# Cross attention's values by seven block products, with the weights' block sums grown in SBUF

## The chip, the core and the metric

The kernel runs on one NeuronCore of a Trainium2 chip, as one program in one launch. The metric is the device time of that launch in microseconds, as a median of several runs. Beside it stands one execution taken by the hardware profiler.

The engines are named as in the profile: PE is the matrix engine (PEld its loading of the stationary operand), DVE the vector engine, ACT the scalar engine, POOL the general engine, SP the engine that here only issues DMAs.

## What is computed

One decoder layer on 256 tokens of width 1024, in float32:

```python
xn = rmsnorm(h, norm_mix_g)
q_a, k_a, v_a, q_b, f_b, i_b, og_b, g_a, g_b = split_cols(xn @ w_in)
y_a = moba_attention(q_a, k_a, v_a, positions) @ w_br_attn
y_b = hgrn2(q_b, f_b, i_b, og_b, lb) @ w_br_hgrn
h = h + (sigmoid(g_a) * y_a + sigmoid(g_b) * y_b) @ w_out
# cross attention with 256 memory tokens, 4 heads of 256
q = rmsnorm(h, norm_x_g) @ wq_x
kv = rmsnorm(mem, norm_mem_g) @ wkv_x          # keys: columns 0 to 1023, values: 1024 to 2047
h = h + (softmax(q k^T / 16) v) @ wo_x
# feed-forward, hidden width 2816
gu = rmsnorm(h, norm_ffn_g) @ w_ffn_in
h = h + (silu(gate) * up) @ w_ffn_out
out = rmsnorm(h, final_norm_g)
```

The change is in the line of `kv` (its values) and in what surrounds it.

## The kernel before

**Precision.** A float32 operand is split into a high part (`hi`, in the format that PE multiplies fast) and the rest (`lo`), and a product is three matmuls: hi by hi, hi by lo, lo by hi. For activations the halves are named `Mh, Ml` (memory), `h1h, h1l` (the normed residual), `oxh, oxl` (what attention gives), for weights `hi, lo`. ACT copies the high part, DVE subtracts it from the raw tile.

**Units of weights.** All weights lie in one array `w` of units of 128 x 2048 (1 MB), in the order of the list `ORDER`. A unit of kind "F" is 256 columns by the full depth of 1024; one of kind "T" is 512 columns by half the depth (`kh` 0 or 1). `prep()` loads the next unit from DRAM into one of three `raw` buffers (its DMA is issued on SP), makes `hi` in two pieces of 1024 on ACT and `lo` in two on DVE; there are three buffers of each. `nxt()` returns the unit that is due and prepares up to two ahead (`LEAD`).

**Products.** `gemm_f` takes an "F" unit: two groups of 16 matmuls that give a feature-major result (`psf`); `gemm_t` takes two "T" units: 2 x 24 matmuls that give both groups of 128 tokens (`pst`). Each ends with `tick()`, which advances background generators (`bg`) by a step, so that the vector work of another part and its few matmuls lie among the big products. PE's instructions run in the order of the program; the order on the other engines is made by a scheduler, except where `keep_in_program_order` or `issue_after` says otherwise.

**Cross attention.** The memory is scaled by its gain and split (`memory()`, tile `M2`) while the attention's output products run. After `w_out` come four chunks of keys (`gemm_f(M2, ...)`, into `kxh, kxl`, the subtraction on POOL), the first half of the values (`gemm_t`, `ev_vx(0)`), four chunks of queries, and the second half of the values (`ev_vx(1)`). One chunk of queries is one head: `scores(x)` gives its scores (`xs`), the softmax on DVE and ACT (`xp`), and two ticks later the turn of the probabilities (`xT`, then `ph, pl`). `pv(x)` multiplies with the values (`xo`, into `ox`). After all four heads come the four units of `wo_x`, for each group of tokens and each half of the columns (`pso`), added to the residual `H` by `add_h2`; then the mean of squares (`rstd_h2`, `hn`), and the turn of the normed residual (`turn_h2`, `h2T`, `h2g`).

**The feed-forward** already computes pairs of its column blocks with seven products of a quarter of the work, in Strassen's manner with Winograd's sums: the products are `P1` to `P7`, in the order `SEVEN`, accumulated in the banks `pqA`, `pqB`, `pqF`, with token sums `SS` made once by `token_sums()`. The weights' sums come from `block_sums()`: one of its steps runs at each tick; SP copies a block to a DRAM tile (`t1`, `t2`, `t3`, `t4`), POOL adds another block by an accumulating DMA (line 743). Its unit's halves are made by `halve()` (lines 1146 and 1151).

Of the kernel before, what the change touches and what calls it, by code (L numbers as in the profile page):

```python
# [42 lines left out]
def plan():  # L43
# [13 lines left out]
    order += tgroup("wkv_x", 1024)[:2]  # L57
    order += [("F", "wq_x", c * 256) for c in range(4)]
    order += tgroup("wkv_x", 1024)[2:]
    order += tgroup("wo_x", 0)  # L60
# [9 lines left out]
SEVEN = ("P1", "P2", "P6", "P7", "P5", "P3", "P4")  # L70

# [22 lines left out]
SPACING = 9  # L94
# [50 lines left out]
def build(tc, A, out):  # L145
    nc = tc.nc
    V, SC, G, PE, SY = nc.vector, nc.scalar, nc.gpsimd, nc.tensor, nc.sync
    with ExitStack() as ctx:
# [46 lines left out]

        def prep(tags=None, raw=None):
# [3 lines left out]
            if raw is None:  # L200
                raw = wr.tile([128, 2048], F32, name="raw", tag="raw")
            if tags is None:
                hi = wh.tile([128, 2048], F32R, name="hi", tag="hi")
                lo = wl.tile([128, 2048], F32R, name="lo", tag="lo")
            else:
                hi = big(tags[0], "hix", (128, 2048), F32R)
                lo = big(tags[1], "lox", (128, 2048), F32R)
# [6 lines left out]
            if sent == 1:  # L214
                SY.dma_start(raw, A["w"][i])
            for c in range(pieces):
# [5 lines left out]
                V.tensor_tensor(lo[:, a], raw[:, a], hi[:, a].bitcast(F32), op=ALU.subtract)  # L222
            ready[i] = (hi, lo)
# [5 lines left out]
        def nxt(lead=LEAD):  # L229
            i = at[0]  # L230
            at[0] += 1
            while made[0] <= min(i + lead, len(ORDER) - 1):
# [74 lines left out]
        def split(src, hi, lo, scale=None):  # L307
            if scale is None:
                SC.activation(hi, src, AF.Copy)
                V.tensor_tensor(lo, src, hi.bitcast(F32), op=ALU.subtract)  # L310
# [426 lines left out]
        def block(q, name):  # L737
            i, kh = {"11": (1, 0), "21": (1, 1), "12": (0, 0), "22": (0, 1)}[name]
            return A["w"][where["I", q + i, kh]]

        def block_sums():
# [8 lines left out]
            for g, q in enumerate(DOUBLES):  # L750
                t1, t2_, t3 = (dr.tile([128, 2048], F32, name="%s_%d" % (z, q)) for z in ("t1", "t2", "t3"))
                scr[q] = {"P5": t1, "P6": t2_, "P7": t3}
                i = SPACING * g
                at_step(i, lambda t=t3, q=q: tc.keep_in_program_order(SY.dma_start(t, block(q, "22"))))
                at_step(i + 6, lambda t=t1, q=q: tc.keep_in_program_order(SY.dma_start(t, block(q, "11"))))
                at_step(i + 4, lambda t=t3, q=q: add(t, q, "12"))
                at_step(i + 10, lambda t=t1, q=q: add(t, q, "12"))
                at_step(i + 8, lambda t=t2_, t3=t3: tc.keep_in_program_order(SY.dma_start(t, t3)))
                at_step(i + 12, lambda t=t2_, q=q: add(t, q, "11"))
                if g == 0:  # L760
                    t4 = dr.tile([128, 2048], F32, name="t4")
                    scr[q]["P4"] = t4
                    at_step(i + 16, lambda t=t4, t2_=t2_: tc.keep_in_program_order(SY.dma_start(t, t2_)))
                    at_step(i + 20, lambda t=t4, q=q: add(t, q, "21"))
# [184 lines left out]

        def memory():  # L950
# [3 lines left out]
            for k in range(8):  # L954
                split(raw[:, k], Mh[:, k], Ml[:, k], gv[:, V_MEM + k:V_MEM + k + 1])
# [11 lines left out]
        mg = memory()  # L967
        start(mg)
# [55 lines left out]
        drain(mg)  # L1024
# [19 lines left out]
        pp = big("P2", "pp", (128, 2, 4, 2, 256), F32R)  # L1044
        ph, pl = pp[:, 0], pp[:, 1]

        def ev_vx(c):
            def ev(t, ps):
                a = slice(c * 512, (c + 1) * 512)
                split(ps, vxh[:, t, a], vxl[:, t, a], mem["r"][:, t:t + 1])  # L1050
            return ev

        gemm_t((Mh, Ml), ev_vx(0))
        drain(h1g)

# [28 lines left out]
        for c in range(4):  # L1084
            gemm_f(H1, ev_sum(qxh, qxl, c))
            g = scores(c)
# [5 lines left out]
        oxh, oxl = ox[:, 0], ox[:, 1]  # L1092

        def pv(x):
# [5 lines left out]
            split(po, oxh[:, 2 * x:2 * x + 2], oxl[:, 2 * x:2 * x + 2])  # L1100

        for x in range(XH):
            for g in sg[:x + 2]:
                drain(g)
            pv(x)
# [400 lines left out]
```

## Time and profile before

| | |
|---|---|
| median of 3 runs | 612.17 us (612.1 to 612.2) |
| the profiled execution | 612.86 us, span 611.1 us |
| granted clock of PE | 0.998 |
| busy PE / PEld | 602.2 / 502.9 us |
| busy DVE / ACT / POOL | 448.9 / 373.1 / 110.0 us |
| HBM | 155.21 MB read, 34.60 MB written |

A row of a group or of the timeline has the start (if it is one instruction), the time, engine and line, the operation, the tiles written and read, shapes and type; in square brackets stands the time for which the engine was idle before it and what ended that. A matmul's time is its length in a pipeline: the next one starts before it ends. In a list of waits the columns are the total in us, how often, and the longest. Times are microseconds from the start of the span.

### The profile page before, as it was taken

Reading aid. Unit: us, or ns where it says so; the run is one execution under the profiler, and the core shown is the slowest. Engines: PE = TensorE matmul, PEld = TensorE weight load, DVE = VectorE, ACT = ScalarE, POOL = GpSimd, SP = SyncE. Lnnn points to the kernel's source line nnn. Section 1 sums busy time; section 2 is a strip of 40 time slices with the busy share of each in tenths; the row PEclk is TensorE's granted clock in tenths of the full one; section 3 lists DMA queues with packets and bytes.
Section 4 is the critical chain, followed back from the end, with each engine's and each line's share of the span. In section 5 each row is a group of like instructions: output and inputs, shape, how many; then the busy total and the mean of one; then the engine's idle time right before and its main releaser. Section 6 shows DMA issues by size and latency. Waiting matters only on the chain.

```text
span 611.1 us, 8304 instructions
## 1 busy us (share of the span) xinstructions
PE 602.2 (99%) x3093; PEld 502.9 (82%) x3093; DVE 448.9 (73%) x702; ACT 373.1 (61%) x603; POOL 110.0 (18%) x137
## 2 busy tenths in 40 slices
PE   8999999999999999999999999999999999999995
PEld 7888888888887887778888888888878888888884
DVE  7598867978756877658866566694896887878953
ACT  7695545333377676736447656684776667677732
POOL 3898100112200431000301403100000000000003
PEclk9999999999999999999999999999999999999999
DMA  8886688747995789957779778863949979796601
GB/s 346 348 305 197 217 252 327 246 139 285 322 257 220 242 260 285 330 203 317 275 216 308 233 280 225 253 215 132 351 158 335 369 267 391 235 383 220 248 2 69
DMA packets 21864, 156.79 MB, mean 257 GB/s; under 512 B 2752, under 2 KB 3392, under 8 KB 5312
## 3 DMA queue, kind: packets, MB, share of 16 engines
q1 hardware_dynamic: 18224, 134.46, 56.7%
q0 software_dynamic: 2880, 20.97, 17.4%
q10 hardware_dynamic: 720, 0.84, 0.4%
q8 instruction: 24, 0.39, 0.3%
q14 instruction: 16, 0.13, 0.1%
HBM read 155.21 MB, written 34.60 MB: 311 GB/s over the span
## 4 chain that ended last, share of the span: by engine, by line
PE 90%; DVE 5%; ACT 2%; issue 1%; POOL 0%; POOLq 0%; DVEq 0%; ACTq 0%
PE pst L262 13%; PE pst L264 13%; PE pst L263 13%; PE pqA L1311 8%; PE psf L283 7%; PE pqF L1311 4%; PE psf L284 4%; PE acc L264 3%; PE acc L263 3%; PE acc L262 3%; PE pqB L1311 2%; PE lp L637 2%; DVE lo L1151 1%; PE psg L538 1%; PE as L826 1%
## 5 line engine op out<-in xcount | busy, mean ns | idle before, releaser
L222 DVE TENSOR_TENSOR lo<-raw,hi 128x1024 fp32r<-128x1024 f32 (+1 forms) x128 | 156.5, 1233 | 56.5 <-ACT hi L221 56.1
L221 ACT ACTIVATE hi<-raw 128x1024 fp32r<-128x1024 f32 (+1 forms) x128 | 129.0, 1028 | 98.5 <-PE pst L264 79.3
L262 PE MATMUL pst<-hi,XX 128*128 128x512 f32 x224 | 90.4, 404 | 0.0
L264 PE MATMUL pst<-hi,XX 128*128 128x512 f32 x224 | 87.4, 390 | 0.0
L263 PE MATMUL pst<-lo,XX 128*128 128x512 f32 x224 | 87.3, 390 | 0.0
L264 PEld LDWEIGHTS pst<-hi,XX 128*128 128x128 f32 x224 | 42.0, 188 | 9.0
L262 PEld LDWEIGHTS pst<-hi,XX 128*128 128x128 f32 x224 | 42.1, 188 | 8.8 <-issue 0.7
L263 PEld LDWEIGHTS pst<-lo,XX 128*128 128x128 f32 x224 | 42.1, 188 | 7.9
L1151 DVE TENSOR_TENSOR lo<-raw,hi 128x2048 fp32r<-128x2048 f32 (+1 forms) x18 | 36.8, 2052 | 10.6 <-ACT hi L1146 10.5
L1146 ACT ACTIVATE hi<-raw 128x1024 fp32r<-128x1024 f32 x32 | 32.0, 1052 | 7.4 <-PE acc L264 5.3
L1151 DVE TENSOR_TENSOR lo<-rawx,hi 128x2048 fp32r<-128x2048 f32 x12 | 27.5, 2288 | 8.1 <-ACT hi L1146 8.1
L1146 ACT ACTIVATE hi<-rawx 128x1024 fp32r<-128x1024 f32 x24 | 24.1, 1051 | 5.9 <-PE acc L264 2.6
L1311 PE MATMUL pqA<-hi,SS 128*128 128x512 f32 x80 | 26.4, 390 | 0.0
L1180 POOL DMA_DIRECT2D b<-t x4 | 3.6, 894 | 124.3 <-DVE fu L1244 124.3
L264 PE MATMUL acc<-hi,hids 128*128 128x512 f32 x62 | 24.3, 392 | 0.7 <-DVE hids L310 0.7
L262 PE MATMUL acc<-hi,hids 128*128 128x512 f32 x62 | 24.4, 393 | 0.0
L263 PE MATMUL acc<-lo,hids 128*128 128x512 f32 x62 | 24.2, 390 | 0.0
L283 PE MATMUL psf<-H,hi 128*128 128x512 f32 x64 | 22.7, 398 | 0.0
L283 PE MATMUL psf<-M,hi 128*128 128x512 f32 x64 | 22.5, 394 | 0.0
L283 PE MATMUL psf<-XX,hi 128*128 128x512 f32 x64 | 22.4, 394 | 0.0
L743 POOL DMA_DIRECT2D t<-w x16 | 13.8, 878 | 46.7 <-DMA t<-w 32.1
L1151 DVE TENSOR_TENSOR lo<-b,hi 128x2048 fp32r<-128x2048 f32 x7 | 16.0, 2292 | 6.2 <-ACT hi L1146 6.2
(418 smaller groups left out, 1511.7 us busy)
## 6 DMA issues: line engine op xcount, KB each, us to landing
raw<-w SPq DMA_DIRECT2D x75, 1024.0 KB, 6.3
t<-w POOLq DMA_DIRECT2D x16, 1024.0 KB, 10.0
raw<-t SPq DMA_DIRECT2D x12, 1024.0 KB, 6.8
rawx<-w SPq DMA_DIRECT2D x10, 1024.0 KB, 7.2
rawx<-t SPq DMA_DIRECT2D x4, 1024.0 KB, 8.9
b<-w SPq DMA_DIRECT2D x4, 1024.0 KB, 9.3
b<-t POOLq DMA_DIRECT2D x4, 1024.0 KB, 8.5
raw<-w SPq DMA_DIRECT2D x4, 512.0 KB, 6.5
```

Of the source, the lines that this page charges most:

```text
L221: SC.activation(hi[:, a], raw[:, a], AF.Copy)
L222: V.tensor_tensor(lo[:, a], raw[:, a], hi[:, a].bitcast(F32), op=ALU.subtract)
L262: PE.matmul(ps, xh, h, start=first, stop=False)
L263: PE.matmul(ps, xh, l, start=False, stop=False)
L264: PE.matmul(ps, xl, h, start=False, stop=last)
L283: PE.matmul(ps, w[0][:, k, a], X2[:, :, k], start=k == 0, stop=False)
L284: PE.matmul(ps[:, 0], w[1][:, k, a], X2[:, 0, k], start=False, stop=k == 7)
L637: PE.matmul(ps[:, j], KS[:, a0 + j], QQ[:, a0 + j], start=True, stop=True)
L743: tc.keep_in_program_order(G.dma_start(t, block(q, name), accum_op=ALU.add, max_dma_last_dim=8192))
L1146: pin(SC.activation(hi[:, a], raw[:, a], AF.Copy))
L1151: pin(V.tensor_tensor(lo[:, a], raw[:, a], hi[:, a].bitcast(F32), op=ALU.subtract))
L1311: PE.matmul(ps, x[k], z[:, k], start=first and k == 0 and i == 0, stop=k == 3 and i == 2, skip_group_check=not first)
```

## The change

The values are computed as the feed-forward computes its pairs: with the 256 memory tokens as two halves, the depth of 1024 as two halves and the columns as two halves, there are seven products of 12 matmuls with 512 columns. The token sums (`SSm`) come from `mem_sums()`. The seven products stand among the key chunks, in the order `CROSS` (numbers 0 to 3 are key chunks, 4 to 7 query chunks); both halves of the values are complete before the first query chunk.

The weights' sums: P1 reads block 11 from a tile of its own (`b11`), to which block 12 is added for P5. A tile `b22` is loaded with block 22 at step 36 of `block_sums()`, gets block 12 at step 38 (P7 reads it), then block 11 after P7's halves are made (P6), then block 21 after P6's (P4). P2 and P3 read blocks 21 and 22. These additions are accumulating DMAs issued by POOL. The memory's scaled copy `mg` is now kept, made by eight more copies on ACT.

The steps of `block_sums()` for the feed-forward follow each other at a spacing of 7 instead of 9 ticks, with other distances inside. After the last query chunk there is no more unit of values: `pv(0)`, `pv(1)`, the scores of the last head, and then output products of the first 128 tokens by heads (`wo_part(t, c, x)`, six matmuls each) alternate with `pv(2)` and `pv(3)`. The first halves for the feed-forward and one low part are ordered behind named instructions (`turned_v`, `behind`).

```diff
+CROSS = (0, "P1", "P7", "P2", 1, "P6", 2, "P5", 3, "P3", "P4", 4, 5, 6, 7)
...
-SPACING = 9
+SPACING = 7
+HOME = (36, 38)
+T4 = (19, 23)
...
+        sums, grow = {}, {"P1": "12", "P7": "11", "P6": "21"}
...
+            if STREAM[i] in ("P1", "P5"):
+                if STREAM[i] == "P1":
+                    sums["1"] = big("B12", "b11", (128, 2048))
+                raw = sums["1"]
+            elif STREAM[i] in ("P7", "P6", "P4"):
+                raw = sums["3"]
...
+            if STREAM[i] in grow:
+                G.dma_start(raw, block("vx", grow[STREAM[i]]), accum_op=ALU.add)
...
-                split(raw[:, k], Mh[:, k], Ml[:, k], gv[:, V_MEM + k:V_MEM + k + 1])
+                SC.activation(mg[:, k], raw[:, k], AF.Copy, scale=gv[:, V_MEM + k:V_MEM + k + 1])
+                split(mg[:, k], Mh[:, k], Ml[:, k])
...
+        def product(ps, x, w, first):
+            xh, xl = x
+            for k in range(4):
+                for i, (x, z) in enumerate(((xh, w[0]), (xh, w[1]), (xl, w[0]))):
+                    PE.matmul(ps, x[k], z[:, k], start=first and k == 0 and i == 0, stop=k == 3 and i == 2,
+                              skip_group_check=not first)
+
+        SSm = big("P2", "SSm", (128, 2, 4, 4, 128), F32R)
+
+        def mem_sums():
+            a11, a12, a21, a22 = (mg[:, 4 * c:4 * c + 4, t * 128:(t + 1) * 128] for t in range(2) for c in range(2))
+            V.tensor_tensor(a22, a22, a21, op=ALU.subtract)
+            V.tensor_tensor(a21, a11, a21, op=ALU.subtract)
+            yield 1
+            put(SSm, 2, a21)
+            yield 1
+            s2 = t2("s2", (128, 4, 128))
+            V.scalar_tensor_tensor(s2, a22, -1.0, a11, op0=ALU.mult, op1=ALU.subtract)
+            V.scalar_tensor_tensor(a12, s2, -1.0, a12, op0=ALU.mult, op1=ALU.subtract)
+            put(SSm, 1, s2)
+            yield 1
+            put(SSm, 0, a22)
+            put(SSm, 3, a12)
...
-        for c in range(4):
-            gemm_f(M2, ev_sum(kxh, kxl, c))
...
-        gemm_t((Mh, Ml), ev_vx(0))
...
+        def cross_product(name):
+            if name == "P6":
+                drain(ms)
+            key = {"P1": "A", "P6": "A", "P5": "A", "P3": "A", "P2": "B", "P7": "F", "P4": "F"}[name]
...
+            product(ps, block_tokens((Mh, Ml), SSm, name), by_k(nxt(), 4), first)
...
+        for u in CROSS:
+            if u in SEVEN:
+                cross_product(u)
+                continue
+            if u < 4:
+                gemm_f(M2, ev_sum(kxh, kxl, u))
+                continue
...
+            gemm_f(H1, ev_sum(qxh, qxl, u - 4))
...
-        gemm_t((Mh, Ml), ev_vx(1))
...
-        for x in range(XH):
-            for g in sg[:x + 2]:
-                drain(g)
-            pv(x)
...
+        pv(0)
+        pv(1)
+        for f in later:
+            f()
+        later.clear()
+        drain(sg[2])
+        run(prep(("P0",)))
...
+        wo_part(0, 0, 0)
+        wo_part(0, 0, 1)
+        pv(2)
+        wo_part(0, 1, 0)
+        wo_part(0, 1, 1)
+        drain(sg[3])
+        with tc.issue_after(turned_v[2]):
+            run(prep(("B12", "B6")))
+        wo.append(by_k(ready.pop(i0 + 3), 4))
+        wo_part(0, 0, 2)
+        pv(3)
+        drain(bs)
+        wo_part(0, 1, 2)
...
-                pin(SC.activation(hi[:, a], raw[:, a], AF.Copy))
+                with tc.issue_after(turned_v[3]) if n == 0 else nullcontext():
+                    pin(SC.activation(hi[:, a], raw[:, a], AF.Copy))
...
-                pin(V.tensor_tensor(lo[:, a], raw[:, a], hi[:, a].bitcast(F32), op=ALU.subtract))
+                with tc.issue_after(behind[n]) if n in behind else nullcontext():
+                    pin(V.tensor_tensor(lo[:, a], raw[:, a], hi[:, a].bitcast(F32), op=ALU.subtract))
...
-                for kh in range(2):
-                    wo_part(ps, t, c, kh)
-                add_h2(t, c, ps)
+                for x in range(0 if t else 3, 4):
+                    wo_part(t, c, x)
+                add_h2(t, c, pso[t, c])
```

More of the change, by code (lines that the diff above doesn't have):

```diff
@@ L56, in plan @@
     order += [("F", "wkv_x", c * 256) for c in range(4)]
-    order += tgroup("wkv_x", 1024)[:2]
+    order += tgroup("wkv_x", 1024)
     order += [("F", "wq_x", c * 256) for c in range(4)]
-    order += tgroup("wkv_x", 1024)[2:]
-    order += tgroup("wo_x", 0)
+    order += [("T", "wo_x", c * 512, kh) for kh in range(2) for c in range(2)]
     for j in range(NF // 2):
@@ L70, with stream @@
 SEVEN = ("P1", "P2", "P6", "P7", "P5", "P3", "P4")
+CROSS = (0, "P1", "P7", "P2", 1, "P6", 2, "P5", 3, "P3", "P4", 4, 5, 6, 7)
+def stream():
+    n = next(n for n, u in enumerate(ORDER) if u[0] == "I")
+    k = [ORDER.index(("F", w, c * 256)) for w in ("wkv_x", "wq_x") for c in range(4)]
+    return list(range(k[0])) + [k[u] if isinstance(u, int) else u for u in CROSS] + list(range(k[7] + 1, n))
+STREAM = stream()
 def ffn_plan():
@@ L1336, in ffn_product @@
             ps = bank_of[key]
-            product(ps, name, w, first)
+            product(ps, block_tokens(X2, SS, name), w, first)
             if name == "P1":
```

163 lines of the change are left out of this document (99 added, 64 removed).

## The prediction

> **What bounds the kernel now.** I read the page's busy times and chain first, then the waits of PE, then PE's timeline around the edit, then the other engines there.
>
> ```profile
> PE 602.2 (99%) x3093; PEld 502.9 (82%) x3093; DVE 448.9 (73%) x702; ACT 373.1 (61%) x603; POOL 110.0 (18%) x137
> PE 90%; DVE 5%; ACT 2%; issue 1%; POOL 0%; POOLq 0%; DVEq 0%; ACTq 0%
> ```
>
> ```profile
> PE warm L359 <- DVE still L356: 1.6, 1, 1.6
> PE acc L264 <- DVE hids L310: 0.7, 1, 0.7
> PE xT L1080 <- DVE xp L1074: 0.2, 1, 0.2
> ```
>
> The first line is busy time by engine, the second the chain of work that ended last, the three others everything that PE ever waited for (total, times, longest). PE is the bound: an edit gains what it takes out of PE's own queue, plus at most the last two waits, and loses whatever new waits it gives PE. The profiled execution took 612.86 us for a span of 611.1; the median of the runs is 612.17. I sum against 612.86 and move the result by the 0.69 between them. About 0.2% (1.2 us) is what a measurement of this kernel can tell from no change.
>
> **The matmuls taken out.** The values `mem @ wkv_x[:, 1024:]` are four units of 24 matmuls; seven products are 12 each.
>
> ```profile
> L262 PE MATMUL pst<-hi,M x32: 387/389/482, 350.4 to 401.1; 128*128 128x512 f32 x32
> L263 PE MATMUL pst<-lo,M x32: 389/389/397, 350.6 to 401.4; 128*128 128x512 f32 x32
> L264 PE MATMUL pst<-hi,M x32: 388/389/397, 350.8 to 401.6; 128*128 128x512 f32 x32
> ```
>
> ```profile
> 463.74 2.72 PE pqA L1311 x12
> 466.46 2.72 PE pqF L1311 x12
> ```
>
> The first three rows are all matmuls of the values: 96. The other two, from the chain, are products of the FFN of the very form the change uses: 12 matmuls take 2.72 us back to back (0.227 each; the 389 ns is the pipelined length of one). 96 - 84 = 12 matmuls: **-2.72 us**, all on the path. The first output products by heads are the same 96 matmuls in another order: 0.
>
> **What the seven products need from DVE and ACT.** In the new order, all of them stand among the keys' chunks, before the first query chunk.
>
> ```profile
> 327.20:361.30 34.10, 34.10 (x188) 29.55 (x187) 20.24 (x29) 20.60 (x36) 9.84 (x10) 1.00 0.86 290
> ```
>
> ```profile
> L222 DVE TENSOR_TENSOR lo<-raw,hi x6: 1216/1222/1228, 380.9 to 397.6; 128x1024 fp32r<-128x1024 f32 x6
> L221 ACT ACTIVATE hi<-raw x6: 1042/1054/1062, 379.8 to 395.7; 128x1024 fp32r<-128x1024 f32 x6
> ```
>
> ```profile
> 359.55 0.75 DVE L313 SCALAR_TENSOR_TENSOR vxl<-pst,r_m,vxh 128x512 fp32r<-128x512 f32 x1
> 437.00 0.69 DVE L1325 TENSOR_TENSOR fc<-pqB,f 128x512 f32<-128x512 f32 x1 [0.36 <-PE pqB L1311]
> 446.82 0.68 DVE L1287 TENSOR_TENSOR SS<-s,SS 128x512 fp32r<-128x512 f32 x1
> ```
>
> The window is that stage before (keys and half of the values): length, then busy PE, PEld, DVE, ACT and POOL. It halves six units; the new stage has eleven, and lasts 34.10 + 36 x 0.227 = 42.3 us. DVE: 20.24 + 10 halves x 1.22 + four `SSm` lows x 0.68 + two token sums and three `fc` x 0.69 + two more `vxl` x 0.75 = 40.1 us. ACT gets ten `hi` x 1.05 and some 6 us of copies: about 37. So PE stays the bound of the stage, but DVE is within 2 us of it. Units are halved two ahead and I find each pair ready by a microsecond or more: 0, with a bound of 2 us above. The extra scale copies of the memory (eight on ACT) lie in the output products of attention, well before their use: 0.
>
> **The sums grown in SBUF.** P7, P6 and P4 read one tile, `b22`, each after one more accumulating load from POOL; P5 reads P1's tile after one. A load cannot be issued before both halves of the product before are made.
>
> ```profile
> 303.23 0.69 DVE L918 SCALAR_TENSOR_TENSOR tat<-tat,pst 128x512 f32<-128x512 f32 x1 [1.12 <-PE pst L264]
> 330.76 1.22 DVE L222 TENSOR_TENSOR lo<-raw,hi 128x1024 fp32r<-128x1024 f32 x1
> 327.20 0.48 PE L283 MATMUL psf<-M,hi 128*128 128x512 f32 x1
> 332.84 1.03 PE L1002 MATMUL h1T<-cst,H 128*128 128x128 f32 x8
> 333.63 0.48 PE L283 MATMUL psf<-M,hi 128*128 128x512 f32 x1
> ```
>
> ```profile
> DMA to landing us min/median/max: 8.0/8.6/11.8
> DMA to landing us min/median/max: 8.2/10.0/21.4
> ```
>
> The last two rows are the times from issue to landing of the FFN's `b` tiles (SBUF, four of the eight accumulated by POOL) and of POOL's accumulating loads into DRAM (L743). The first row is the end of attention's output products: from there `b22`'s home is free and its load goes out on SP (behind it the copy of `t2_9`, P1's block and P2's weights, none needed until the keys' stage is near). It lands near 312, and POOL's add near 322; behind that add on POOL stands `r_m`, which wants only its issue, at 312. P7's halving waits for a buffer until 327.2 anyway. P7 takes the place of the old second key chunk, whose second low ended at 330.76 + 1.22 = 332: there the load for P6 goes out. On PE a key chunk is 5.64 us (327.20 to 332.84), the transposes 0.79, so P6 begins at 333.63 + 3 x 2.72 + 5.64 = 347.4 and needs its first halves (1.05 + 1.22) before: the load must land by 345.1, 13.1 us after issue. With 8.6 there are 4.5 us to spare, with 11.8 still 1.3: 0. P4 and P5 have over 10 us to spare. The Trainium skill, page DMA: Bandwidth & Descriptors, section Anatomy of one DMA — SWDGE (gpsimd) path, fits such a transfer at 2.0 us plus its bytes over 436 GB/s, 4.4 us for this one as an estimate, and would leave 8.7 to spare; the trace's shortest is 8.0, so the measurement decides.
>
> The FFN's own sums move closer together (`SPACING` 9 to 7) and end sooner; they lie in DRAM and are read from 431 on: 0. The chunk loads keep three buffers, and SP mostly waits for those.
>
> ```profile
> SPq L215 <- DVE lo L222: 234.1, 40, 8.9
> ```
>
> **The end of cross attention.** Before, the last two units of values covered the softmax of heads 2 and 3; now products with V and output products by heads do.
>
> ```profile
> 387.10 0.28 PE L262 MATMUL xs<-kxh,qxh 128*128 128x256 f32 x1
> 388.53 0.60 PE L1080 MATMUL xT<-cst,xp 128*128 128x128 f32 x4
> 388.88 0.48 PE L262 MATMUL pst<-hi,M 128*128 128x512 f32 x1
> 401.59 0.39 PE L264 MATMUL pst<-hi,M 128*128 128x512 f32 x1
> 402.16 0.81 PE L1080 MATMUL xT<-cst,xp 128*128 128x128 f32 x4 [0.19 <-DVE xp L1074]
> 402.73 0.37 PE L257 MATMUL xo<-pp,vxh 128*128 128x256 f32 x1
> 408.58 0.40 PE L262 MATMUL pso<-hi,ox 128*128 128x512 f32 x1
> 392.85 0.62 DVE L1074 TENSOR_SCALAR xp<-xp,xsum 128x256 f32<-128x256 f32 x2
> 407.33 0.60 ACT L309 ACTIVATE ox<-xo 128x512 fp32r<-128x512 f32 x1 [0.66 <-PE xo L259]
> 422.06 1.34 ACT L1202 ACTIVATE hn<-H,r 128x512 f32<-128x512 f32 x2 [0.93 <-POOL r L1198]
> 424.92 1.04 PE L1211 MATMUL h2T<-cst,hn 128*128 128x128 f32 x8
> 411.44 2.28 DVE L1151 TENSOR_TENSOR lox<-raw,hix 128x2048 fp32r<-128x2048 f32 x1
> 431.48 1.06 ACT L1146 ACTIVATE px<-raw 128x1024 fp32r<-128x1024 f32 x1 [2.28 <-PE pso L264]
> 457.70 0.69 DVE L310 TENSOR_TENSOR hids<-hidT,hids 128x512 fp32r<-128x512 f32 x1
> ```
>
> Scores of a head take 1.43 us (387.10 to 388.53), a turn 0.35, a product with V (402.73 to 408.58) / 4 = 1.46. Today's stall is 402.73 - (401.59 + 0.23) = 0.91 less the turn's 0.35: **-0.56**, gone with the unit it waits behind. What is late next, step by step:
> - A head's softmax ends at 392.85 + 0.62, 4.9 us after its scores (388.53), with a 1.22 us half of weights between. Head 2's turn comes after 0.35 + 1.46 + 1.46 + 1.43 = 4.7 us and no weights are left to halve there: 0. Head 3 has 0.35 + 2.72 + 1.46 + 2.72 = 7.2: 0. The product with V of head 1 starts 1.46 us after its turn and wants a copy and a subtraction (0.60 + 0.68) and their hand-over: +0.1.
> - Head 3's output halves have only six matmuls (1.36 us) of cover; 0.60 + 0.68 of work, behind one 1.06 of ACT for the FFN's weights that waits for the same V: **+0.35** (0 to 1.2).
> - Both sums of the first 128 tokens now end 1.36 us apart, and FFN halves that were made earlier stand among them on DVE (1.22, then 2.28 ahead of the mean). Before, `hn` was ready at 422.06 + 1.34 = 423.4 and PE turned it at 424.92, 1.5 us to spare; I put it 1.9 later: **+0.4** (0 to 1.5).
> - The second half of `px` (1.06 on ACT, it waits for the last output product) now goes ahead of the last square, so the second turn of h and the token sums come about 0.75 later. From there DVE is packed until 457.70, which is what PE's 0.7 waits for: that becomes 1.45, **+0.75** (-0.7 to +1.5).
>
> Sum: -2.72 - 0.56 + 0.1 + 0.35 + 0.4 + 0.75 = **-1.7 us**: 611.2 against the profiled 612.86, **610.5** as a median.
>
> **The rivals.**
> 1. *The tail closes.* Were the list's four costs nil and the 0.7 gone too, it would be -2.72 - 0.56 - 0.7 = -4.0: 608.2. For it: all four are short hand-overs. Against: DVE's packed stretch before 457.70.
> 2. *DVE becomes the bound of the stage of the keys.* Its lows meet POOL's `kxl` subtractions:
>
> ```profile
> 336.36 1.78 POOL L1037 TENSOR_TENSOR kxl<-kx,kxh 128x256 fp32r<-128x256 f32 x1 [2.77 <-ACT kxh L1036]
> 375.96 1.75 DVE L222 TENSOR_TENSOR lo<-raw,hi 128x1024 fp32r<-128x1024 f32 x1
> ```
>
> Here a low took 1.75 instead of 1.22; the stage has eight `kxl`, so 8 x 0.53 = 4.2 us more at worst, 44.3 of DVE in 42.3 of PE: 2 us lost, 612.5. Against it: in the first row, among the keys, it was POOL that was held. The Trainium skill, page SBUF — State Buffer, section SBUF: two separate sides, has the rule: a DVE instruction with two SBUF inputs and a GpSimd one that reads SBUF want the same read interface, and the first holds it to its end. The two rows agree, each side held once; the rule speaks against a change that adds ten lows beside these subtractions.
> 3. *The chain through SBUF is late (slower).* P6's load can't go out before 332 and follows P1's load and near the last FFN sums on the same queue. From 13.1 us to landing each further microsecond is PE's; from 16.0 us on the kernel is slower than 613.4, and at the 21.4 seen at L743 it would be 8.3 later: 618.8. Against: loads into SBUF took at most 11.8.
> 4. *It saves nothing.* The changed program's order of instructions has seven groups of 12 in place of the 96, so I give this no chance.
>
> **How the numbers follow.** Forecast 0.50 (609.5 to 611.5), rival 1 0.18, rival 2 0.18 (611.5 to 613), rival 3 0.14. Faster by over 1.2 us (below 610.95): 0.38 of the forecast, rival 1 and 0.03 of rival 2: 0.59. Slower (above 613.4): rival 3 and 0.03 of rival 2: 0.17. Between: 0.24. The range 608.3 to 613.0 leaves out rival 3 and a little at either end.
>
> **What would show it.** Right: seven groups of 12 at about 2.72 each; no PE wait on them; a wait of PE for `hids` of 1 to 2 us and short ones for `ox` and `hn`. Wrong: PE waiting for `hi` or `lo` of `b22` (rival 3), for lows of key chunks (rival 2), or for none at all (rival 1).

## The result, and the profile after

The changed kernel takes 617.37 us (median of 6 runs, 615.96 to 618.73), against 612.18 of before in the same series (612.02 to 612.61): a ratio of 1.0083 (95%: 1.0067 to 1.0098). It is 5.2 us slower, where 1.7 faster was forecast, and 4.4 above the end of the range (613.0). The profiled execution took 616.46 us for a span of 614.5, 0.9 below the median of its kernel, while before's lay 0.7 above; so the two traces show 3.6 of the 5.2.

From the page of the changed kernel, busy time by engine and the chain of work that ended last:

```profile
PE 602.2 (98%) x3081; PEld 499.7 (81%) x3081; DVE 463.9 (76%) x720; ACT 384.5 (63%) x624; POOL 119.5 (19%) x141
PE 79%; DVE 7%; DMA 6%; issue 4%; ACT 2%; POOL 1%; SPq 0%; POOLq 0%; DVEq 0%; ACTq 0%
```

PE has its 12 matmuls less, but only 79% of the chain in place of 90: DVE and DMA have come in. The waits of PE (us in total, times, longest), without the unchanged first one:

```profile
PE acc L295 <- DVE hids L340: 1.4, 1, 1.4
PE h2T L1352 <- ACT hn L1343: 1.3, 1, 1.3
PE xT L1190 <- DVE xp L1184: 0.6, 1, 0.6
PE xo L289 <- DVE pp L340: 0.4, 1, 0.4
PE psi L293 <- ACT H L1355: 0.2, 1, 0.2
```

Before had two of these, of 0.7 and 0.2. From PE's timeline, the starts of the third and of the fourth group of matmuls in the stage of the keys (start, length):

```profile
336.00 0.39 PE L1083 MATMUL pqF<-hi,SSm 128*128 128x512 f32 x1
...
338.72 0.39 PE L1083 MATMUL pqB<-hi,M 128*128 128x512 f32 x1
```

A product of 12 matmuls takes 338.72 - 336.00 = 2.72 us, as costed. I add up the distances between the starts of neighbouring PE instructions by what they write, from the first key chunk (327.20 before, 326.73 after) to the end:

| PE's time on, us | before | after | difference | forecast |
|---|---|---|---|---|
| values (96 matmuls, then 84), with the old stall | 22.42 | 19.25 | -3.17 | -3.28 |
| chunks of keys and queries (`psf`) | 44.95 | 45.93 | +0.98 | 0 |
| scores, to the turn (`xs`) | 5.74 | 6.49 | +0.75 | 0 |
| products with V (`xo`) | 5.85 | 6.73 | +0.88 | +0.1 |
| output products (`pso`) | 21.91 | 23.01 | +1.10 | +0.35 |
| both turns of h (`h2T`) | 1.58 | 2.05 | +0.47 | +0.4 |
| wait before the second turn (for `hn`) | 0 | 1.46 | +1.46 | 0 |
| first FFN units (`psi`) | 10.98 | 11.74 | +0.76 | 0 |
| wait for `hids` | 0.84 | 1.54 | +0.70 | +0.75 |
| sum | | | +3.93 | -1.68 |

Together with an opening that ended 0.47 earlier this is, to 0.1, the 3.4 us between the spans. (19.25 is the sum of the seven groups of 12.) The gain is there to 0.1 us; what failed is what it was to cost. Four places show it.

**Among the keys.** The windows from 300 to 345 (length, busy PE, PEld, DVE, ACT, POOL, granted clock, DMA share, GB/s), before first,

```profile
300.00:345.00 45.00, 45.00 (x238) 38.46 (x237) 29.39 (x41) 24.64 (x44) 11.59 (x12) 1.00 0.82 254
```

then after:

```profile
300.00:345.00 45.00, 45.00 (x227) 37.94 (x226) 31.07 (x42) 25.61 (x42) 9.02 (x10) 1.00 1.00 314
```

The mean share of the DMA engines is 1.00 over these 45 us. The load on which P6 rests, and the timeline of ACT and DVE behind it (in brackets: idle before, and what ended it):

```profile
L253 POOL DMA_DIRECT2D b<-w x1: 906/906/906, 332.6 to 332.6; - x1
DMA to landing us min/median/max: 10.5/10.5/10.5
```

```profile
343.25 2.01 ACT L250 ACTIVATE hi<-b 128x1024 fp32r<-128x1024 f32 x2 [3.82 <-DMA b<-w]
344.34 1.23 DVE L251 TENSOR_TENSOR lo<-b,hi 128x1024 fp32r<-128x1024 f32 x1 [2.59 <-ACT hi L250]
...
350.82 1.22 DVE L251 TENSOR_TENSOR lo<-raw,hi 128x1024 fp32r<-128x1024 f32 x1
...
387.41 1.06 ACT L250 ACTIVATE both<-raw 128x1024 fp32r<-128x1024 f32 x1 [1.12 <-DMA raw<-w]
388.64 0.59 ACT L1180 ACTIVATE xp<-xp,xmx,r 128x256 f32<-128x256 f32 x1
```

The load took 10.5 us where 13.1 were allowed: P6 is in time. But ACT takes its work in order, stood 3.82 us in front of that load, and so did everything queued behind it: the halves of the next key chunk (number 2, the third; the expectations below call it the second) were ready only while PE was in that chunk (the low at 350.82; PE starts a matmul 0.25 and 0.30 late there). Later the same happens at the output weights: `both` waits for its load, the exponentials of a head stand behind it, and PE waits 0.6 for that head (`xp`).

**The last head.** From ACT's timeline:

```profile
414.69 1.06 ACT L1287 ACTIVATE hix<-raw 128x1024 fp32r<-128x1024 f32 x1 [2.31 <-PE xo L289]
415.66 0.58 ACT L340 ACTIVATE ox<-xo 128x512 fp32r<-128x512 f32 x1
```

The half of 1.06 that waits for the same product with V goes first, and the copy that PE waits for second.

**The second root.** Timeline rows of DVE, POOL and ACT before,

```profile
433.39 0.21 DVE L1196 TENSOR_SCALAR v<-ssq 128x1 f32<-128x1 f32 x1 [0.85 <-ACT hjunk L1193]
434.34 2.29 DVE L1151 TENSOR_TENSOR px<-raw,px 128x2048 fp32r<-128x2048 f32 x1 [0.73 <-ACT px L1146]
433.68 0.56 POOL L1198 TENSOR_TENSOR r<-v,nhalf 128x1 f32<-128x1 f32 x1 [11.66 <-DVE v L1196]
```

and after:

```profile
434.85 0.22 DVE L1335 TENSOR_SCALAR v<-ssq 128x1 f32<-128x1 f32 x1 [0.85 <-ACT hjunk L1332]
434.98 2.28 DVE L1293 TENSOR_TENSOR px<-raw,px 128x2048 fp32r<-128x2048 f32 x1
435.14 2.54 POOL L1339 TENSOR_TENSOR r<-v,nhalf 128x1 f32<-128x1 f32 x1 [11.39 <-DVE v L1335]
437.71 1.33 ACT L1343 ACTIVATE hn<-H,r 128x512 f32<-128x512 f32 x2 [2.90 <-POOL r L1339]
```

Before, the subtraction of `px` was late (its second half came behind the last square on ACT), and the root on POOL slipped in ahead of it: 0.56 us. After, both halves of `px` are early, and the subtraction, queued right behind `v`, starts 0.16 us before the root; the root, one number per partition, lasts 2.54 us, to 0.4 us after the subtraction's end. `hn` and PE pay for that.

**The last sum of h.** Rows of DVE and ACT after, just ahead of that `v`:

```profile
431.10 2.29 DVE L1293 TENSOR_TENSOR lo<-raw,hi 128x2048 fp32r<-128x2048 f32 x1 [2.04 <-ACT hi L1287]
434.09 0.63 ACT L1332 ACTIVATE hjunk<-H 128x512 f32<-128x512 f32 x1 [0.30 <-DVE H L1331]
```

`v` comes 3.3 us after the first FFN product (431.58), where it was 2.1 before. The halves of `px` are not the reason: ACT had done both and stood idle for 0.30 us when the input of the last square came. DVE's low of 2.29, which waited 2.04 us for its `hi`, stands ahead of that input, the last sum of h.

### The profile page after: what moved, and what is told of

Its sections match the earlier page's. It is cut to its first block, busy times and chain, and to the rows that moved or that the text cites. A ratio compares the mean times of both kernels' runs of the same rounds, so it can differ in the third digit from the quotient of the medians.

```text
span 614.5 us, 8337 instructions
## 1 busy us (share of the span) xinstructions
PE 602.2 (98%) x3081; PEld 499.7 (81%) x3081; DVE 463.9 (76%) x720; ACT 384.5 (63%) x624; POOL 119.5 (19%) x141
## 4 chain that ended last, share of the span: by engine, by line
PE 79%; DVE 7%; DMA 6%; issue 4%; ACT 2%; POOL 1%; SPq 0%; POOLq 0%; DVEq 0%; ACTq 0%
PE pst L293 11%; PE pst L295 11%; PE pst L294 11%; PE pqA L1083 8%; PE psf L314 5%; DMA b<-w 5%; PE pqF L1083 4%; PE acc L295 3%; PE acc L293 3%; PE acc L294 3%; PE psf L315 2%; PE pqB L1083 2%; PE lp L667 2%; PE psg L568 1%; DVE lo L251 1%
## 5 line engine op out<-in xcount | busy, mean ns | idle before, releaser
L251 DVE TENSOR_TENSOR lo<-raw,hi 128x1024 fp32r<-128x1024 f32 (+1 forms) x124 | 151.8, 1235 | 38.5 <-ACT hi L250 38.1
L250 ACT ACTIVATE hi<-raw 128x1024 fp32r<-128x1024 f32 (+1 forms) x124 | 124.3, 1027 | 85.8 <-PE pst L295 74.9
L1083 PE MATMUL pqA<-hi,SS 128*128 128x512 f32 x80 | 26.3, 390 | 0.0
L295 PE MATMUL acc<-hi,hids 128*128 128x512 f32 x62 | 24.3, 391 | 1.4 <-DVE hids L340 1.4
L1287 ACT ACTIVATE hi<-b 128x1024 fp32r<-128x1024 f32 x14 | 14.1, 1054 | 8.9 <-PE acc L295 4.5
```

The source lines that it names most:

```text
L250: SC.activation(hi[:, a], raw[:, a], AF.Copy)
L295: PE.matmul(ps, xl, h, start=False, stop=last)
L1083: PE.matmul(ps, x[k], z[:, k], start=first and k == 0 and i == 0, stop=k == 3 and i == 2, skip_group_check=not first)
L1287: pin(SC.activation(hi[:, a], raw[:, a], AF.Copy))
```

## The experiments

Times are medians; each ratio is against runs of before in the same series. Series differ by up to 0.8 us in before, so kernels of different series are compared by their ratios.

| kernel | us | ratio (95%) |
|---|---|---|
| the change | 617.37 | 1.0083 (1.0067 to 1.0098) |
| root ahead of px | 615.32 | 1.0045 (1.0032 to 1.0058) |
| no adding loads | 614.39 | 1.0033 (1.0021 to 1.0046) |
| tail alone | 616.50 | 1.0070 (1.0057 to 1.0084) |
| old spacing | 626.84 | 1.0233 (1.0219 to 1.0247) |
| root and ACT orders | 613.71 | 1.0008 (0.9990 to 1.0027) |
| ... and unit 9 behind the tail | 614.00 | 1.0027 (1.0017 to 1.0037) |
| root, ACT orders, weights' home | 613.10 | 0.9997 (0.9983 to 1.0012) |
| ... and unit 9 among the products with V | 610.93 | 0.9968 (0.9958 to 0.9978) |
| ... its last add ahead of the first root | 612.87 | 1.0004 (0.9992 to 1.0017) |
| tail alone, mended | 612.94 | 1.0007 (0.9998 to 1.0016) |
| the best again | 611.14 | 0.9982 (0.9973 to 0.9991) |
| the change, unit 9 moved | 614.60 | 1.0040 (1.0026 to 1.0053) |

**The root ahead of px.**

```diff
-            if t:
-                behind[3] = v.ins
             G.tensor_tensor(r2[:, t:t + 1], v2[:, t:t + 1], nhalf[:, :1], op=ALU.pow)
+            if t:
+                behind[3] = V.tensor_copy(r2seen, r2[:, t:t + 1]).ins
```

> The changed kernel, but the low half of px waits for the root: DVE reads r2 once (a [128,1] copy) behind the power on POOL, and the subtraction of px (2.28 us) is queued behind that copy in place of behind the mean v. Theory (the pow on POOL took 2.54 us in place of 0.56 because DVE's subtraction ran beside it): r is back at 0.6 us, hn starts 1.5 to 1.8 us earlier, PE's wait of 1.46 us before the second turn of h goes, time 615.6 to 616.1 against 617.4 for the change. Rival (DVE is packed to the first hids anyway): the wait for hn goes but the one for hids grows by as much, time 617 to 617.5.

615.32 us. Timeline rows of DVE and POOL, then the longest of PE's waits in this kernel, without the first:

```profile
436.10 0.21 DVE L1336 TENSOR_SCALAR v<-ssq 128x1 f32<-128x1 f32 x1 [0.85 <-ACT hjunk L1333]
436.99 0.15 DVE L1340 COPY r2seen<-r 128x1 f32<-128x1 f32 x1 [0.67 <-POOL r L1338]
436.39 0.56 POOL L1338 TENSOR_TENSOR r<-v,nhalf 128x1 f32<-128x1 f32 x1 [11.42 <-DVE v L1336]
```

```profile
PE acc L295 <- DVE hids L340: 1.3, 1, 1.3
PE xT L1190 <- DVE xp L1184: 0.7, 1, 0.7
PE psf L315 <- DVE lo L251: 0.6, 1, 0.6
```

The root is back at 0.56, the wait for `hn` is gone, and that for `hids` has not grown. 2.0 us of the 5.2 are the edit that put the subtraction of `px` behind `v`; the rows of PE at the tail give the same 2.0 (1.5 before the second turn, 0.2 within it, 0.3 in the first FFN units). In this run the wait in key chunk 2 is large enough to be listed (`psf`, for a low of weights).

**Without the adding loads.**

```diff
-            if STREAM[i] in grow:
-                G.dma_start(raw, block("vx", grow[STREAM[i]]), accum_op=ALU.add)
...
-            at_step(HOME[1], lambda: G.dma_start(sums["3"], block("vx", "12"), accum_op=ALU.add))
```

> The changed kernel without the four accumulating loads of cross attention's weights: P7, P6 and P4 read the block 22 as loaded, P5 the block 11, so the values come from the wrong weights; all else stays. Theory (the chain of sums in SBUF, through waits of ACT and DVE in front of the second key chunk, costs 0.5 to 1.3 us, and part of the spread of the runs): the 0.55 us in which PE waits in the second key chunk go, 616.1 to 616.9, and the runs lie closer. Rival (the sums land in time and are free): 617.4 as the change. A third (they cost the whole loss, 5 us): 612.5.

614.39 us, and five runs within 0.8 us, where the change's six spread over 2.8. PE's waits, without the first and one of 0.2 at the tail (`psi`):

```profile
PE acc L293 <- DVE hids L338: 1.4, 1, 1.4
PE h2T L1349 <- ACT hn L1340: 1.3, 1, 1.3
```

The waits for `xp`, `pp` and in key chunk 2 are gone, and only those of the tail are left. So the loads cost about 3 us, more than the 0.5 to 1.3 I gave the chain, though not the whole.

**The tail alone.** Before's units of values, in one piece between keys and queries, with the changed end; without the memory's scale copies and token sums, and with the FFN's sums at their old steps.

```diff
-CROSS = (0, "P1", "P7", "P2", 1, "P6", 2, "P5", 3, "P3", "P4", 4, 5, 6, 7)
+CROSS = (0, 1, 2, 3, "V0", "V1", 4, 5, 6, 7)
...
-            if u in SEVEN:
-                cross_product(u)
+            if isinstance(u, str):
+                gemm_t((Mh, Ml), lambda t, ps, c=int(u[1]): ev_vx(t, c, ps))
                 continue
```

> Before's four units of values (96 matmuls, between the keys and the queries; no block sums, no token sums, the sums of the FFN at their old steps) with the changed end of cross attention: products with V and output products by heads, px ahead of the last square. If the loss is the tail's alone (its waits in the profile of the change: about 0.6 for the turn of a head, 0.7 at the products with V, 0.7 at the last head, 1.7 at hn, 0.8 at the second half of h, 0.7 at hids, less 0.6 of before), this takes 612.2 + 4.6 = 616.8. If the loss is that of the seven products, it takes 612 or a little less (611.6, the old stall gone).

616.50 us: the changed end costs 3.8 to 4.3 by itself. That is near the expected 4.6, but the 4.6 had in it the wait at the turn of a head, which is not here. The two longest waits behind the first are those of the kernel without the adding loads:

```profile
PE acc L299 <- DVE hids L344: 1.3, 1, 1.3
PE h2T L1349 <- ACT hn L1340: 1.3, 1, 1.3
```

The tail's loss and the loads' loss are set against the products' gain: by the ratios 4.3 + 3.1 - 2.7 = 4.7 us, against 5.1 for the change, within what the intervals allow.

**The FFN's sums at their old steps.**

```diff
-SPACING = 7
+SPACING = 9
...
-T4 = (19, 23)
+T4 = (16, 20)
...
-                at = [i + n for n in (0, 4, 2, 6, 10, 15)]
+                at = [i + n for n in (0, 4, 6, 10, 8, 12)]
```

> The changed kernel with the FFN's block sums at their old steps (spacing 9 and the old offsets). Theory (the closer sums crowd the DMA engines from 300 to 345, where landings took 15 to 20 us in place of 10): landings there fall below 13 us, PE's wait in the second key chunk goes, 616.5 or less. Rival (the crowd is only moved to 345 to 365 and holds the output weights): 617.4 or more.

626.84 us, 9.5 slower than the change: the rival, and far beyond it. PE's waits, P6's load from issue to landing, and the windows behind P6's start:

```profile
PE pqA L1083 <- ACT SSm L1069: 5.7, 1, 5.7
PE xT L1190 <- DVE xp L1184: 2.9, 1, 2.9
```

```profile
DMA to landing us min/median/max: 18.9/18.9/18.9
```

```profile
346.00:352.60 6.60, 1.00 (x6) 0.62 (x4) 1.41 (x2) 2.49 (x4) 0.00 (x0) 0.78 1.03 283
352.60:356.50 3.90, 3.82 (x9) 2.77 (x10) 3.90 (x6) 3.76 (x7) 0.90 (x1) 0.50 0.60 168
```

At the old steps three adding loads and a plain one of the FFN's sums go out between 304 and 338, among the chain in SBUF, where the change has one and a copy; the load takes 18.9 us, and PE waits 5.7 for P6 (named after `SSm`, which had its place behind the load on ACT). This is the third rival of the prediction to a tenth: it put what exceeds 13.1 us on PE, and 18.9 - 13.1 = 5.8. (The tenth is in part luck: the load went out at 331.1 and not at 332, and 2.7 us passed from its landing to P6 and not 2.3.) What it did not have is the second window: after that wait the granted clock is 0.50 for 3.9 us. So the closer steps, which the prediction held to be worth nothing, save 9.5 us.

**Two orders on ACT.** (`squared` is the list of the squares of h, kept in `add_h2`.)

```diff
-                with tc.issue_after(turned_v[3]) if n == 0 else nullcontext():
+                front = turned_v[3] if n in (0, 4) else squared[-1] if n == 3 and c else None
+                with tc.issue_after(front) if front else nullcontext():
```

> The kernel in which px waits for the root, with two more orders on ACT as they were before the change: the second half of px behind the last square, and the first half of the FFN's fifth unit (hix) behind the copy of the last head's output. Theory (each half of 1.05 us on ACT ahead of a short step costs PE that much): PE's wait for the last head's output (0.7 us, put at 0.35 in the prediction) falls to 0.1 or less, the mean v and with it hn and the token sums come 0.8 earlier, and PE's wait for hids falls from 1.5 to about 0.8: 614.0, 1.3 less than with the root alone (615.3). Rival (the halves put back delay the lows on DVE by as much, and hids waits for those): ox as said, hids unchanged, 614.7.

613.71 us, a ratio of 1.0008 for 1.0045. The 0.7 us that PE lost at the last head is gone, but `hids` waits 1.4 as in the change: the theory for `ox`, and the rival's outcome for `hids`. Of the 2.3 us between the two profiles 1.1 lie at the tail (0.9 in the output products, 0.2 in the first turn of h) and 1.0 in the chunks of keys and queries, which this edit does not touch (46.5 us in the kernel without it, 45.4 here, 45.9 in the change): that part is not the edit's. DVE's timeline in this kernel shows why `hids` did not move:

```profile
430.01 2.29 DVE L1294 TENSOR_TENSOR lo<-raw,hi 128x2048 fp32r<-128x2048 f32 x1 [1.43 <-ACT hi L1288]
432.22 0.68 DVE L1333 TENSOR_TENSOR H<-pso,H 128x512 f32<-128x512 f32 x1
433.76 0.22 DVE L1338 TENSOR_SCALAR v<-ssq 128x1 f32<-128x1 f32 x1 [0.85 <-ACT hjunk L1334]
```

The same rows in a later kernel, the one with the weights' home moved:

```profile
427.40 2.29 DVE L1295 TENSOR_TENSOR lo<-raw,hi 128x2048 fp32r<-128x2048 f32 x1 [0.17 <-ACT hi L1289]
429.61 0.69 DVE L1334 TENSOR_TENSOR H<-pso,H 128x512 f32<-128x512 f32 x1
431.14 0.21 DVE L1339 TENSOR_SCALAR v<-ssq 128x1 f32<-128x1 f32 x1 [0.85 <-ACT hjunk L1335]
```

The window from 445 to 458 of before (DVE's busy time is the third figure of the row after the length):

```profile
445.00:458.00 13.00, 12.76 (x59) 10.21 (x57) 13.00 (x13) 9.42 (x14) 0.00 (x0) 1.00 0.38 138
```

and of the kernel with the two orders:

```profile
445.00:458.00 13.00, 12.45 (x57) 9.96 (x55) 13.00 (x13) 9.80 (x15) 0.00 (x0) 1.00 0.36 139
```

DVE is busy for 13.00 of 13.00 us in both. From its first `lox` (438.02 before, 438.39 here) to `hids` (457.70, 458.07) its work takes 19.68 us in both kernels (19.67 or 19.68 in every trace here), so the time of `hids` is set by the start of that stretch; and the start follows `v`. The order of the halves of `px` on ACT is not what delays `v`: it comes 3.3 us after the first FFN product with either order. In the kernel with the two orders a low of 2.29 stands ahead of the last sum of h, because its `hi` waited for a buffer: the change keeps the second output weights there, which PE reads to the last product.

**Unit 9's sums behind the tail.** The kernel above, with the three copies and three adding loads of the FFN's last unit taken out of the keys' stage.

```diff
-                steps.setdefault(i, []).append(f)
+                steps.setdefault(i, []).append(f) if q != 9 else late.append(f)
...
         drain(bs)
+        for f in late[:2]:
+            f()
...
         hn1 = rstd_h2(1)
+        for f in late[2:4]:
+            f()
...
+            for f in {6: late[4:5], 9: late[5:]}.get(n, ()):
+                f()
```

> The kernel above, with the FFN's last block sums (three copies and three adding loads for unit 9) taken out of the stages of the keys and put behind the tail: two loads before the last output product, two adds behind the last root, the copy and its add among the FFN's products. Theory (the adding loads of cross attention are late because they share the DMA engines with the FFN's sums): b22's loads land within 10 us, PE's 0.55 to 1.1 us in the second key chunk and 0.6 to 0.8 at the turn of a head go: 1.5 to 2 us less than without this, 612.0 to 612.5. Rival (the four adding loads are late by themselves, each behind the halving of the product before): the waits stay, and the time too.

614.00 us. The waits of the keys' stage are gone as the theory said, and the time is not: another is there.

```profile
PE hidT L1404 <- DVE fu L1395: 1.5, 1, 1.5
PE acc L295 <- DVE hids L340: 1.4, 1, 1.4
```

The two adds, issued at 434.52 and 435.12, took 12.8 and 21.3 us to land beside the FFN's own loads, which landed up to 7.8 later than without them (451.83 for 444.05). The crowd was moved, not removed.

**The output weights' second unit in P0** (a tile of its own; in place of the third; else the kernel with the ACT orders).

```diff
+WO1 = STREAM.index(ORDER.index(("T", "wo_x", 512, 0)))
...
+            if i == WO1:
+                both = big("P0", "both", (128, 4096), F32R)
+                hi, lo = both[:, 0:2048], both[:, 2048:4096]
...
-        run(prep(("P0",)))
+        run(prep())
```

> The kernel with the ACT orders of before, and the output weights' second unit in P0 in place of the third (so the two units that stay in the rotating buffers are both of the first column half, which PE has done with one product earlier). Theory (DVE is packed from its first low of the FFN to the first hids, in all kernels for 19.7 us, and starts that stretch when v is made; v is late because a low of 2.29 us that waited for ACT, and ACT for a buffer that PE freed, stands ahead of the last sum of h): the halves of the third FFN unit are made 3 us earlier, v comes 2.1 us after the first FFN product starts in place of 3.3, hids and the end come 1.1 earlier: 612.6 against 613.7 without. Rival (PE's own lateness in the stages before sets the end): no change, 613.5 to 614.

`v` comes 2.1 us after the first FFN product (429.06) in place of 3.3, and the wait for `hids` is 0.6. The median, 613.10, is within what the ratios can tell (0.9997 for 1.0008): the wait is shown gone, the time not resolved. The runs spread over 3.7 us (610.78 to 614.50).

**Unit 9's sums among the products with V.** Two loads ahead of the first product with V, two adds behind the second, the copy later among the output products, the last add behind the first root; the other edit is the first of the diff for the sums behind the tail.

```diff
+        for f in late[:2]:
+            f()
         pv(0)
         pv(1)
+        for f in late[2:4]:
+            f()
...
         drain(bs)
+        late[4]()
...
                 hn0 = rstd_h2(0)
+                late[5]()
```

> The kernel above, with the FFN's last block sums (unit 9) taken out of the keys' stages and put among the products with V and the output products, where the DMA engines are 11% busy: two loads and two adds near 385 to 400, the copy between, the last add behind the first root. Theory (crowding of the DMA engines from 300 to 345 delays the halves of the second key chunk and of the output weights): the 1.3 us of waits there go without the wait of 1.5 us that the same sums caused when they lay in the FFN's start, so 1.3 to 1.6 less than without this: 611.0 to 611.4, faster than before. Rival (DVE's packed stretch sets the end whatever PE does ahead of it, since its start follows the output products, which follow PE): half of it, 612.

610.93 us, ratio 0.9968: 1.9 faster than before, 2.2 less than without this. All that PE waits for besides its start (a third line, 0.2, lies in the opening):

```profile
PE acc L296 <- DVE hids L341: 1.4, 1, 1.4
```

**The last add earlier.**

```diff
+                late[5]()
                 hn0 = rstd_h2(0)
-                late[5]()
```

> The kernel with unit 9's sums among the products with V, its last adding load ahead of the first root on POOL in place of behind it. Theory (what is left of the wait for hids, 1.4 us, comes from that load: issued at 421.98 it landed at 432.92, beside the FFN's first loads, whose halves on ACT kept DVE's packed stretch waiting 1.16 us): the load goes out near 414.5, the stretch starts 0.8 earlier, hids waits 0.6: 610.1 to 610.4 against 610.9. Rival (the pow on POOL then waits for the copy and the load, and hn is late): 611.5 or more. Third: no change, 610.9.

612.87 us: neither theory's time. The root did not wait (0.57 us); but the load, from 413.27 to 423.10, now met the FFN's first loads (one landed at 424.61 in place of 422.57), their halves stood ahead of the sums of h, and `v` came 3.9 us after the first FFN product. The wait for `hids` stayed at 1.3.

**The tail alone, mended**: the kernel of the tail alone, with the three diffs for the root, the ACT orders and the weights' home.

> Before's four units of values (no block products) with the changed end of cross attention and the three mends of it: px behind the root, the two ACT orders, the output weights' second unit in P0. Theory (the loss of the tail was these three orders, 616.5 with none of them): PE's waits of before go but the one for hids, 612.0 to 612.5, equal to before, so that 1.1 to 1.6 of the 2.72 us of the products are left in the kernel with everything mended (610.9). Rival (the order by heads costs by itself): 613.5 or more.

612.94 us, ratio 1.0007: equal to before, so the order by heads costs nothing once these orders are mended. Against this kernel the block products, with everything mended, bring 0.25 to 0.39% (0.9982 and 0.9968 for 1.0007, of two series of the same kernel): 1.5 to 2.4 of their 2.72 us.

**The best once more**, unchanged.

> The mended kernel once more, unchanged (orders of ACT and DVE at the tail mended, unit 9's sums among the products with V): if 610.9 stands, 610.5 to 611.3 and 1.2 to 2.2 below before. If the lower time was of that one series, 612 to 613, as the kernel with the last add moved.

611.14 us, ratio 0.9982 (0.9973 to 0.9991): faster than before again, by 1.1 us where it was 1.9 in the first series. In this profile the wait for `hids` is 0.7, for 1.4 in the first one of the same kernel.

**The change with unit 9 moved alone**: the edits of unit 9 among the products with V, and no other.

> The changed kernel with only unit 9's block sums moved among the products with V; px's order, the ACT orders and the output weights' homes as the change has them. Theory (crowding of the DMA engines among the keys costs the change 2 to 3 us, as leaving the adding loads out did: 614.4): 614.4 to 615.4, the waits in the second key chunk, at the turn of a head and at the products with V gone, those behind the tail (hn 1.5, H 0.7, hids 1.4) left. Rival (those waits are covered by the tail's own): 617.

614.60 us, what leaving the adding loads out gave (614.39), with the real sums in place. PE's waits, without the first and the last, and the stage's window:

```profile
PE acc L295 <- DVE hids L340: 1.3, 1, 1.3
PE h2T L1361 <- ACT hn L1352: 1.3, 1, 1.3
PE xo L289 <- DVE pp L340: 0.3, 1, 0.3
```

```profile
300.00:345.00 45.00, 45.00 (x226) 37.90 (x225) 33.42 (x47) 27.88 (x46) 10.04 (x10) 1.00 0.94 277
```

The DMA share from 300 to 345 is 0.94, for 1.00 in the change and 0.83 without the adding loads. So 2.6 to 2.8 us of the change's loss come from the FFN's sums and the cross attention's adding loads meeting, and not from either alone: taking out either one gives the same time.

## Why the prediction was wrong, step by step

Two steps carry most of the miss. The sums grown in SBUF were put at 0 and cost 2.6 to 2.8 us, as they met the FFN's sums on the DMA engines; the subtraction of `px` behind `v` was not costed at all and cost 2.0.

- **The matmuls and the old stall**, -2.72 and -0.56: right, -3.17 on PE. The window "42.3 us of PE" for the stage of the keys was 43.3.
- **The sums "0", the closer steps "0"**: this failed, by 1.7 us in the profile (`psf` and `xs`) and 2.6 to 2.8 in the medians. I asked whether P6's load lands in time (it does, by 2.6 us) and let only P6 depend on it. Two things were left out: ACT takes its queue in order, so every half behind that load waits with it; and the DMA engines, at 0.82 from 300 to 345 before, had no room for three of the four adding loads of 1 MB and the FFN's sums at their new steps. I took landing times of before as given, when the change itself sets them. (The closer steps are not at fault by themselves: at the old ones it is 9.5 us worse.)
- **Rival 3** had the mechanism and its price right (5.8 for a load of 18.9), but in the kernel as changed it decides at the neighbours of P6, not at P6. **Rival 2** did not come about: no wait of PE names a low of weights that POOL held, and DVE was busy for 34.7 of the stage's 43.3 us, where I had counted 40.1. **Rival 1** was the opposite of what the tail did.
- **The products with V**, +0.1: 0.9 in the profile. 0.6 of it goes when the adding loads are out of the way (`xo` takes 6.13 there, 5.85 before), so most of it was not the hand-over that I costed. With unit 9 moved 0.3 of the wait stays, and which step ahead of `pp` was late is not shown.
- **The last head**, +0.35 (0 to 1.2): 0.7 of wait; the 1.1 of the row also has the 0.15 of the next point. The half of 1.06 was named, and then given a third of its length; with it behind the copy 0.9 of the row came back.
- **hn of the first 128 tokens**, +0.4: right, 0.15 ahead of the first turn and 0.23 within it.
- **px ahead of the last square**, +0.75 on `hids`: +0.70 was measured, and that is luck. The term was the second half of `px` on ACT ahead of the last square; ACT was idle before that square, and `v` was late behind a low on DVE that waited for its `hi` (3.3 us after the first FFN product with either order on ACT, 2.1 with the weights' home moved). And the step did not look at the other edit there, the subtraction of `px` queued behind `v`, nor at who reads `v` next: POOL. That is the largest single wait that the prediction did not have, 1.46 us. I had the rule in hand, and used it only for `kxl`. The Trainium skill, page SBUF — State Buffer, section SBUF: two separate sides, says that a DVE instruction with two SBUF inputs and a GpSimd one that reads SBUF take one read interface whole, whichever starts first; here DVE started 0.16 us first and a root of 0.56 us lasted 2.54. The trace agrees. The subtraction's 2.28 us, added to the forecast of -1.7, would have made it +0.6, about no change; mended alone, the edit gave back 2.0.
- **The first FFN units**, which had no term: +0.76. 0.3 of it goes with the root ahead of `px`, the rest with the weights' home moved (10.98 as before).
- **DVE's packed stretch** before `hids` was read (rival 1 names it) but not used as what it is: 19.7 us from its first `lox` to `hids` in every trace. From `v` to `hids` it is 24.3 us before and in most kernels with the root at 0.56, and 26.3 where the subtraction of `px` stands behind `v`. As PE waits for `hids` in every kernel here, by 0.6 us or more, what makes `v` later behind the output products is PE's in full.

What stays open: eight of the thirteen kernels spread over 2.0 to 3.7 us between executions, before too (2.9 in the series of the weights' home), and one profile shows one execution (that kernel's took 610.78, the shortest of its twelve, for a median of 613.10). What makes the difference from run to run was not tried.

## What to carry to other kernels

Before an edit is costed at nothing because its load is in time, list what stands behind that load's first reader on an engine that works in order, and add the edit's loads to the DMA share of that stage: from 0.82 the three adding loads and the moved sums took it to 1.00 here, and plain loads there took 17 to 21 us to land. Where an order is written out by hand, look at every engine that reads the instruction it is put behind; here a subtraction of 2.28 us on DVE, right behind the input of a POOL step of 0.56, made that step last 2.54, and one DVE read of POOL's result (0.15 us) in front of it took that away. Where an engine is packed from one event to the next, as DVE for 19.7 us here, look for what starts the stretch. And where a term comes out at its forecast size, check that its cause is the one forecast.

## What the runs showed of the hardware

- After a wait of 5.68 us, PE's matmuls of P6 were granted a clock of 0.50 for 3.9 us; P6 took 4.70 us in place of 2.72. The wait cost 7.7 us, not 5.7. After the wait of 2.9 us in the same kernel, the window 400 to 404 had 0.61 (0.50 from 400.9 to 404.3). The Trainium skill, page TensorE: Matmul & The Clock Gate, section Part 1: The HAM clock gate (the "warmup" mystery), puts the drop to half rate behind an idle window of about 3.4 us. The first wait was longer than that, but the clock fell 2.7 us into it (PE idle from 347.0, the clock at 0.50 from 349.7); the second was shorter, and the clock fell all the same. So here less than 3.4 us without work was enough. The waits of 1.3 to 1.5 us for `hn`, `hids` and `fu` did not lower it (1.00 in the windows behind them).
- An adding load of 1 MB from POOL into SBUF took 10.5 us with the DMA engines full and 18.9 with more of the FFN's sums on the same stretch. In the changed kernel, plain loads of 1 MB issued between 303.6 and 318.6 took 17 to 21 us, where those issued from 370 to 383 took 4.7 to 5.3.
